# Moving the low-half subtraction of split weights from GpSimd to VectorE in a hybrid transformer block

## The chip, the cores and the metric

The kernel runs on 1 core of one Trainium2 chip. The metric is the device time of one execution in microseconds; of several runs the median counts. Each engine (TensorE for matrix products, VectorE, ScalarE, GpSimd, and the queues that start DMAs) works through its own list of instructions in order and waits on semaphores for the others.

## What is computed

One layer of a diffusion backbone over 512 latent tokens and 256 context tokens with model width 1024, in float32: a modulated RMS norm, one wide input projection that feeds two mixers, a merge, and a mixture of 16 experts. Cut to what matters:

```python
h_c = modulate(ctx, norm1_g, mod_c[0], mod_c[1]);  h_x = modulate(x, norm1_g, mod_x[0], mod_x[1])
qkv_c, z_c, al_c, be_c, cq_c, ckv_c, kr_c, gt_c = split(h_c @ w_in)     # and the same for h_x
# A: short convolution on q, k, v, then a gated delta rule in chunks, both directions, 8 heads
m = where(strict, einsum(k_beta, k) * decay, 0);  t_inv = triangular_solve(m + eye, eye)
# B: latent attention; k and v of all 768 tokens come from rms_norm(c_kv) @ w_ukv, queries from rms_norm(c_q) @ w_uq
x_mid = x + mod_x[2] * ((sigmoid(g_a) * (y_a @ w_out_a) + sigmoid(g_b) * (y_b @ w_out_b)) @ w_o)
out = x_mid + mod_x[5] * expert_choice_moe(modulate(x_mid, ...), router_w, w_gate, w_up, w_down)
```

## The kernel before

**The split.** Up to the router the matrix products keep float32 precision with operands in a reduced type (fp32r): a weight `raw` is split into a high half `wh` (a copy rounded to fp32r) and a low half `wl` (`raw` minus `wh`), and `mm3` (L139 to L142) makes three products of them, `wh` by high input, `wh` by low input, `wl` by high input. `load_split` (L332 to L339) does it for one weight tile of 128 x 1024 elements: a DMA from the SP queue brings `raw` (L336), ScalarE writes `wh` (L337), and L338 writes `wl` on the engine `lo_eng`, or on GpSimd where none is given. The tags `raw`, `whi` and `wlo` have two buffers each, so at most two weights are on their way, and the ScalarE copy of the next but one waits until TensorE has finished with the oldest.

**Who calls it.** `proj` (L521) calls it without an engine, and stands behind `head_k`, `head_q`, `head_v`, `head_z` (eight heads each) and `spill` (the compressed query `cq`, three tiles, the compressed key `ckv`, two, and the merge gates `gt`, sixteen). The first four weights (`k0`, `q0`, `v0`, `k1`) are split by `split_first` (L372) instead, on a GpSimd pinned by name. `load_wkv` (L1110) calls `load_split` without an engine, four times. `branch` (L1404) calls it with `nc.vector`. `load_wq` (L1101) has a GpSimd subtraction of its own. The weight of decays and rotary keys, `abw`, is split at L518 and L519.

**Order.** The program is written as generators (jobs), one for each head and step. `_Emit.step` (L102) runs them by rank and by a planner's estimates of cost and latency, and so sets the order in which instructions are traced; the tile framework then fixes the order on each engine before the run, and the chip keeps it. In the delta-net stage three kinds of job are mixed: projections with convolution (`conv`, L615: on VectorE one product at L623 and four multiply-adds at L626 for each segment, then SiLU on ScalarE at L628, then transposes on TensorE at L635), the chunk preparation (`decay` and `use`, L746 to L782), the inverse of the triangular matrices (`inverse`, L795: 31 steps of L811 and L813 on VectorE, two transposes, then TensorE at `pY`), and the scan over chunks (`scan`, L912, whose VectorE steps are L934, L957, L977, L987, L989). The projections of the gates `gt` and of `z` fill TensorE in between. The attention follows, then the merge and the output projection, then the experts (L1698 to L1788), which stream all expert weights from memory.

Of the kernel before, what the change touches and what calls it, by code (L numbers as in the profile page):

```python
# [11 lines left out]
F32 = mybir.dt.float32  # L12
# [162 lines left out]
def hybrid_block(ctx: ExitStack, tc: tile.TileContext, I, out, dbg=None):  # L175
    nc = tc.nc
# [70 lines left out]
    abw = gp.tile([P, KT, 96], F32, name="abw")  # L247
# [84 lines left out]
    def load_split(src, kt, m, name, lo_eng=None, tiles=None):  # L332
        raw, wh, wl = tiles or (st.tile([P, kt, m], F32, tag="raw", name=f"raw_{name}", **RAW),
                                st.tile([P, kt, m], F32R, tag="whi", name=f"wh_{name}", **WB),
                                st.tile([P, kt, m], F32R, tag="wlo", name=f"wl_{name}", **WB))
        issued[name] = nc.sync.dma_start(raw, src).ins  # L336
        nc.scalar.activation(wh, raw, AF.Copy)  # L337
        (lo_eng or nc.gpsimd).tensor_sub(wl, raw, wh.bitcast(F32))  # L338
        return wh, wl  # L339

    em = _Emit()
# [174 lines left out]
    abh = st.tile([P, KT, 96], F32R, tag="whi", name="abh")  # L516
    abl = st.tile([P, KT, 96], F32R, tag="wlo", name="abl")
    nc.scalar.activation(abh, abw, AF.Copy)  # L518
    nc.gpsimd.tensor_sub(abl, abw, abh.bitcast(F32))  # L519

    def proj(c0, m, name, ctx_=False, w=None):  # L521
        pl = None
        if name in first:
            w, pl = first[name]
        wh, wl = w or load_split(w_in[:, :, c0:c0 + m], KT, m, name)
        begun = pl is not None
        pl = pl if begun else pmm([P, 512], f"pl_{name}")
        pc = pmm([P, 256], f"pc_{name}") if ctx_ else None
        for k in range(KT, KT) if begun else range(KT):
            mm3(nc, pl[:m], wh[:, k], wl[:, k], hx(k, 0), hx(k, 1), k == 0, k == KT - 1)  # L530
            if k % 2:
                yield 1.3, 0, None
        if ctx_:
            for k in range(KT):
                mm3(nc, pc[:m], wh[:, k], wl[:, k], hc(k, 0), hc(k, 1), k == 0, k == KT - 1)
                if k % 4 == 3:
                    yield 1.3, 0, None
        return pl, pc
# [571 lines left out]
    def load_wkv(p):  # L1110
        WKV[p] = load_split(w_ukv[:, :, p * 512:(p + 1) * 512], 2, 512, f"ukv{p}")
        held.append(p)
# [291 lines left out]
    def branch(i, nm, Y, dt, gr):  # L1404
        if not PRM["sl"]:
            nc.scalar.activation(gr, gr, AF.Sigmoid)
        wh, wl = load_split(I[f"w_out_{nm}"][0].rearrange("(k p) c -> p k c", p=P)[:, :, dt * P:(dt + 1) * P],
                            KT, P, f"wo{nm}{dt}", nc.vector if PRM["wv"] or dt % 2 else nc.gpsimd,
                            spare if (nm, dt) == ("a", PRM["da"]) else None)
        yield 0, 2, None  # L1410
        if PRM["sl"]:
            nc.scalar.activation(gr, gr, AF.Sigmoid)
        pa = pmm([P, SEQ], f"pm{nm}{dt}")
        for k in range(KT):
            y = Y[k // 2][:, k % 2]
            mm3(nc, pa, wh[:, k], wl[:, k], y[:, 0], y[:, 1], k == 0, k == KT - 1)
            if k % 2:
                yield 1.3, 0, None
        return pa
# [393 lines left out]
```

## Time and profile before

| | us |
|---|---|
| median of 3 runs | 1807.21 |
| lowest, highest of them | 1804.39, 1810.33 |
| the profiled execution, its own time | 1812.11 |
| its span, first to last instruction | 1810.4 |

Busy shares of the span: TensorE 89%, VectorE 49%, ScalarE 33%, GpSimd 21%. The span falls into a first part up to about 66 us (loads, norms, first weights), the delta-net stage with the projections up to about 720 us, the attention up to about 930 us, the merge and output projection up to about 1065 us, output and routing up to about 1170 us, and the experts. In the names of the profile PE is TensorE, PEld its weight loads, DVE is VectorE, ACT ScalarE and POOL GpSimd. A number in square brackets behind an instruction is the idle time of its engine just before it, with what ended it.

### The profile page before, as it was taken

How to read it: one execution, taken by the hardware profiler on the slowest of the kernel's cores; microseconds unless marked ns; L12 is line 12 of the kernel's file. 1: busy time of each engine (PE TensorE's matmuls, PEld its weight loads, DVE VectorE, ACT ScalarE, POOL GpSimd, SP SyncE). 2: the span in 40 equal slices, each digit the busy share in tenths (PEclk: the TensorE clock that was granted, in tenths of full speed). 3: DMA queues.
4: the chain of work that ended last, by engine and by line, in shares of the span. 5: the costliest groups of instructions: out<-in, count | busy, mean ns of one | idle time of the engine just before them, and what ended most of it. 6: DMA issues, size and time to landing. Idle time of an engine off the chain costs nothing.

```text
span 1810.4 us, 25319 instructions
## 1 busy us (share of the span) xinstructions
PE 1609.5 (89%) x9990; PEld 1107.8 (61%) x9990; DVE 887.6 (49%) x1903; ACT 593.6 (33%) x1336; POOL 380.2 (21%) x380
## 2 busy tenths in 40 slices
PE   5898998898789998699979897999999999999897
PEld 4676797777677787567867785544454444444343
DVE  3677956965896962557774436212122121222122
ACT  4557337425635343456665424100010000000000
POOL 2443433323333423421230442000000000000000
PEclk8999998999989998899989999999999999999999
DMA  9111311243221342131024972799999999999997
GB/s 311 50 47 47 88 42 47 70 143 115 51 73 53 87 156 60 53 102 46 7 88 137 300 258 116 282 414 388 413 384 414 412 413 413 413 414 412 414 413 301
DMA packets 168409, 382.31 MB, mean 211 GB/s; under 512 B 10373, under 2 KB 91491, under 8 KB 168291
## 3 DMA queue, kind: packets, MB, share of 16 engines
q1 hardware_dynamic: 163328, 372.98, 55.6%
q10 hardware_dynamic: 4963, 7.72, 1.3%
q8 instruction: 78, 1.28, 0.3%
q14 instruction: 40, 0.33, 0.1%
HBM read 366.51 MB, written 14.16 MB: 210 GB/s over the span
## 4 chain that ended last, share of the span: by engine, by line
PE 55%; DVE 20%; DMA 9%; ACT 7%; POOL 4%; issue 4%; SPq 0%; ACTq 0%; DVEq 0%; POOLq 0%
PE pd L1765 8%; PE pg L1724 6%; PE pu L1724 5%; DMA wd<-in_w_down_dram 4%; PE pg L1725 3%; DVE tmp L811 3%; PE pu L1725 2%; DVE cy L626 2%; DVE inv L813 2%; DVE qk L626 2%; PE pc L1781 2%; PE pxe L1667 1%; PE pY L170 1%; DVE qv L626 1%; PE pxe L1668 1%
## 5 line engine op out<-in xcount | busy, mean ns | idle before, releaser
L1724 PE MATMUL pg<-w_gate,XE 128*64 128x320 f32 x496 | 183.4, 522 | 0.0
L1724 PE MATMUL pu<-w_up,XE 128*64 128x320 f32 x480 | 159.6, 487 | 2.2 <-DMA w_up<-in_w_up_dram 2.2
L1725 PE MATMUL pg<-w_gate,XE 128*64 128x320 f32 x496 | 161.2, 465 | 0.0
L1745 DVE TENSOR_TENSOR hd<-hd,pu 128x320 f32<-128x320 f32 (+1 forms) x48 | 18.7, 416 | 288.9 <-PE pu L1725 271.7
L1765 PE MATMUL pd<-wd,hd 128*64 128x512 f32 x668 | 152.3, 603 | 1.9 <-DMA wd<-in_w_down_dram 1.9
L1725 PE MATMUL pu<-w_up,XE 128*64 128x320 f32 x480 | 153.9, 444 | 0.0
L1770 ACT ACTIVATE yo<-hd 128x512 fp32r<-128x512 f32 x16 | 10.1, 629 | 342.7 <-DVE hd L1769 342.7
L1724 PEld LDWEIGHTS pu<-w_up,XE 128*64 128x64 f32 x480 | 64.8, 137 | 72.4 <-issue 39.6
L1765 PEld LDWEIGHTS pd<-wd,hd 128*64 128x64 f32 x668 | 45.2, 137 | 86.0 <-issue 78.5
L1724 PEld LDWEIGHTS pg<-w_gate,XE 128*64 128x64 f32 x496 | 67.9, 144 | 47.6 <-issue 28.9
L1725 PEld LDWEIGHTS pg<-w_gate,XE 128*64 128x64 f32 x496 | 61.6, 143 | 24.2 <-issue 11.2
L1743 ACT ACTIVATE hd<-pg 128x320 f32<-128x320 f32 (+1 forms) x48 | 16.5, 378 | 174.9 <-PE pg L1725 174.9
L1781 PE MATMUL pc<-yo 64*128 64x512 f32 x256 | 47.5, 457 | 26.0 <-ACT yo L1770 22.7
L1781 PEld LDWEIGHTS pc<-yo 64*128 64x128 f32 x256 | 23.3, 194 | 67.4 <-ACT yo L1770 35.9
L1785 DVE TENSOR_TENSOR xm<-xm,pc 128x512 f32<-128x512 f32 x72 | 45.9, 682 | 33.7 <-PE pc L1781 33.7
L811 DVE TENSOR_TENSOR tmp<-inv 128x31 f32<-128x31 f32 (+15 forms) x124 | 60.5, 488 | 2.1
L1769 DVE SCALAR_TENSOR_TENSOR hd<-pd,gs,m 128x512 f32<-128x512 f32 x16 | 12.0, 750 | 96.4 <-PE pd L1765 96.4
L626 DVE SCALAR_TENSOR_TENSOR cy<-cx_v,CW,cy 128x510 f32<-128x510 f32 (+3 forms) x64 | 55.6, 886 | 0.2
L140 PE MATMUL pl_gt<-ht,wh_gt 128*128 128x512 f32 x128 | 53.8, 420 | 0.0
L142 PE MATMUL pl_gt<-ht,wl_gt 128*128 128x512 f32 x128 | 51.6, 404 | 2.3 <-POOL wl_gt L338 2.3
L1671 ACT ACTIVATE XE<-pxe,mod,gs 128x256 f32<-128x256 f32 x32 | 16.3, 561 | 113.6 <-PE pxe L1668 101.0
L813 DVE TENSOR_TENSOR inv<-inv,tmp 128x31 f32<-128x31 f32 (+15 forms) x124 | 51.3, 413 | 2.2
(623 smaller groups left out, 4324.3 us busy)
## 6 DMA issues: line engine op xcount, KB each, us to landing
w_gate<-in_w_gate_dram SPq DMA_DIRECT2D x60, 1408.0 KB, 16.2
w_up<-in_w_up_dram SPq DMA_DIRECT2D x60, 1408.0 KB, 17.9
wd<-in_w_down_dram SPq DMA_DIRECT2D x45, 1536.0 KB
aw<-in_ada_w_dram SPq DMA_DIRECT2D x32, 512.0 KB, 5.4
wd<-in_w_down_dram SPq DMA_DIRECT2D x15, 1024.0 KB, 14.0
aq<-in_ada_w_dram SPq DMA_DIRECT2D x8, 1024.0 KB, 9.5
raw_gt<-in_w_in_dram SPq DMA_DIRECT2D x16, 512.0 KB, 3.9
ring_w<-in_w_up_dram SPq DMA_DIRECT2D x3, 1408.0 KB, 11.9
```

The lines of the kernel that those rows point to most:

```text
L140: nc.tensor.matmul(out, wh, xh, start=first, stop=False)
L142: nc.tensor.matmul(out, wl, xh, start=False, stop=last)
L170: return self._tc.keep_in_program_order(f(*a, **kw))
L626: nc.vector.scalar_tensor_tensor(y[:, o + a:o + b], x[:, o + a + j - 2:o + b + j - 2], w(j), y[:, o + a:o + b], op0=OP.mult, op1=OP.add)
L811: nc.vector.tensor_mul(tv, R[:, j + 1:32, j:j + 1].to_broadcast([P, n, j + 1]), X[:, j:j + 1, 0:j + 1].to_broadcast([P, n, j + 1]))
L813: nc.vector.tensor_sub(X[:, j + 1:32, 0:j + 1], X[:, j + 1:32, 0:j + 1], tv)
L1724: nc.tensor.matmul(dst[c][0:64, :n], x_, w[kk][:, o:o + n], start=(k == ko[0]), stop=(k == ko[3] + 1))
L1725: nc.tensor.matmul(dst[c][64:128, :320], x_, w[kk][:, FA + c * 320:FA + c * 320 + 320], start=(k == ko[0]), stop=(k == ko[3] + 1))
L1745: nc.vector.tensor_mul(hd[pr, o:o + b - a], hd[pr, o:o + b - a], pu[c][pr, a:b])
L1765: nc.tensor.matmul(pd[64 * dh:64 * dh + 64], l_, w[:, j, dh * 512:(dh + 1) * 512], start=(i == 0), stop=(i == 10))
L1781: nc.tensor.matmul(pcs[dh], o_[ps_, t, :], y_[ps_, l, :], start=(i + l == 0), stop=(i + l == len(ys_)))
L1785: nc.vector.tensor_add(xm[t][:, sl], xm[t][:, sl], pcs[dh])
```

## The change

The engine for the low half is VectorE instead of GpSimd where `load_split` is given none, and for `abl`:

```diff
@@ load_split
         issued[name] = nc.sync.dma_start(raw, src).ins
         nc.scalar.activation(wh, raw, AF.Copy)
-        (lo_eng or nc.gpsimd).tensor_sub(wl, raw, wh.bitcast(F32))
+        (lo_eng or nc.vector).tensor_sub(wl, raw, wh.bitcast(F32))
         return wh, wl
@@
     nc.scalar.activation(abh, abw, AF.Copy)
-    nc.gpsimd.tensor_sub(abl, abw, abh.bitcast(F32))
+    nc.vector.tensor_sub(abl, abw, abh.bitcast(F32))
```

## Rows read from the trace of the kernel before

**Rows 1.** The page: busy us by engine; VectorE's busy tenths in 40 slices.

```profile
PE 1609.5 (89%) x9990; PEld 1107.8 (61%) x9990; DVE 887.6 (49%) x1903; ACT 593.6 (33%) x1336; POOL 380.2 (21%) x380
...
DVE  3677956965896962557774436212122121222122
```

**Rows 2.** The page: the chain that ended last, by engine.

```profile
PE 55%; DVE 20%; DMA 9%; ACT 7%; POOL 4%; issue 4%; SPq 0%; ACTq 0%; DVEq 0%; POOLq 0%
```

**Rows 3.** Busy time by stage: columns are named in the first line.

```profile
core 0: us, PE busy (x) PEld busy (x) DVE busy (x) ACT busy (x) POOL busy (x), PEclk, DMA share, GB/s
...
66.00:720.00 654.00, 582.20 (x4434) 486.91 (x4432) 476.21 (x1062) 312.53 (x732) 240.67 (x257) 0.94 0.25 75
...
1170.00:1811.00 641.00, 589.09 (x3204) 276.85 (x3202) 140.35 (x292) 37.30 (x85) 0.00 (x0) 0.97 1.00 401
```

**Rows 4.** Line 338 on GpSimd: durations in ns, shortest/median/longest, first and last start.

```profile
L338 POOL TENSOR_TENSOR wl_gt<-raw_gt,wh_gt x16: 2346/2406/3347, 326.3 to 623.2; 128x1024 fp32r<-128x1024 f32 x16
```

**Rows 5.** Groups of VectorE instructions of line 338: busy, mean ns, idle before.

```profile
L338 DVE TENSOR_TENSOR wl_wob<-raw_wob,wh_wob 128x1024 fp32r<-128x1024 f32 x8 | 11.5, 1436 | 11.1 <-ACT wh_wob L337 11.1
...
L338 DVE TENSOR_TENSOR wl_woa<-raw_woa,wh_woa 128x1024 fp32r<-128x1024 f32 x7 | 9.3, 1328 | 12.7 <-ACT wh_woa L337 12.7
```

**Rows 6.** Line 338 alone in the delta-net stage, busy on DVE and POOL.

```profile
66.00:720.00 654.00, 0.00 (x0) 124.51 (x50) 0.94 0.25 75
```

**Rows 7.** Timeline of GpSimd, the subtractions of 310 to 331 us: start, duration.

```profile
310.45 2.47 POOL L338 TENSOR_TENSOR wl_q<-raw_q,wh_q 128x1024 fp32r<-128x1024 f32 x1
...
320.82 2.40 POOL L338 TENSOR_TENSOR wl_v<-raw_v,wh_v 128x1024 fp32r<-128x1024 f32 x1 [7.90 <-ACT wh_v L337]
326.32 2.42 POOL L338 TENSOR_TENSOR wl_gt<-raw_gt,wh_gt 128x1024 fp32r<-128x1024 f32 x1 [3.10 <-ACT wh_gt L337]
```

**Rows 8.** Timeline of VectorE in the same stretch.

```profile
310.60 2.87 DVE L626 SCALAR_TENSOR_TENSOR cy<-cx_v,CW,cy 128x510 f32<-128x510 f32 x1
...
320.88 2.42 DVE L813 TENSOR_TENSOR inv<-inv,tmp 128x60 f32<-128x60 f32 x1
...
326.43 2.60 DVE L626 SCALAR_TENSOR_TENSOR qk<-cx_k,CW,qk 128x255 f32<-128x255 f32 x1
...
329.16 0.47 DVE L626 SCALAR_TENSOR_TENSOR qk<-cx_k,CW,qk 128x255 f32<-128x255 f32 x1
```

**Rows 9.** VectorE, the first and the last prolonged instruction of the stage.

```profile
69.38 2.06 DVE L623 TENSOR_SCALAR qv<-cx_q,CW 128x512 f32<-128x512 f32 x1
...
637.06 2.41 DVE L842 COPY W<-inv 32x192 f32<-32x192 f32 x1
```

**Rows 10.** VectorE by line: durations in ns, shortest/median/longest.

```profile
L626 DVE SCALAR_TENSOR_TENSOR cy<-cx_v,CW,cy x64: 468/737/2919, 78.5 to 515.0; 128x510 f32<-128x510 f32 x16, 128x511 f32<-128x511 f32 x16, 128x254 f32<-128x254 f32 x16, 128x255 f32<-128x255 f32 x16
...
L813 DVE TENSOR_TENSOR inv<-inv,tmp x124: 190/360/2648, 173.4 to 627.7; 128x31 f32<-128x31 f32 x8, 128x60 f32<-128x60 f32 x8, 128x87 f32<-128x87 f32 x8, 128x112 f32<-128x112 f32 x8
...
L775 DVE SCALAR_TENSOR_TENSOR W<-GH,bp,D x96: 331/340/352, 133.1 to 568.0; 128x128 f32<-128x128 f32 x96
```

**Rows 11.** TensorE's waits from 66 to 720 us: total us, times, longest.

```profile
PE ptn_k L635 <- ACT qk L628: 10.0, 5, 3.2
PE ptn_v L635 <- ACT cy L628: 7.4, 4, 2.4
PE pY L168 <- DVE inv L819: 6.8, 3, 4.1
...
PE pl_z L142 <- POOL wl_z L338: 4.5, 2, 3.3
...
PE ptn_q L635 <- ACT qv L628: 3.4, 2, 2.9
...
PE pl_gt L142 <- POOL wl_gt L338: 2.3, 1, 2.3
PE pl_v L142 <- POOL wl_v L338: 1.9, 1, 1.9
```

**Rows 12.** Timeline of TensorE, the wait that closes the stretch of rows 7 and 8.

```profile
331.19 0.48 PE L635 MATMUL ptn_k<-cst,qk 128*128 128x128 f32 x1 [3.06 <-ACT qk L628]
```

## The prediction

> **What bounds the kernel now.** I read the page first. TensorE is busy 89% of the span, VectorE 49%, GpSimd 21%, and the digits show that VectorE's load lies in the first half [rows 1]. In the chain of work that ended last TensorE has 55%, VectorE 20%, GpSimd 4% [rows 2]: an engine that is busy half the time carries a fifth of the end, one that is moved away from carries little. The busy times by stage say where [rows 3]. The experts (1170 us to the end, 641 us) have 1.00 DMA share, TensorE 589 us and no GpSimd at all: nothing of the change happens there, and they start when the work before them is done. The delta-net stage (66 to 720 us, 654 us) has TensorE busy 582 us, VectorE 476, GpSimd 241. So TensorE is idle for 72 us of this stage, and since its order is fixed, what the stage can gain is what these 72 us give back. The list of TensorE's waits says who makes them [rows 11]: mostly results of the convolution on VectorE (10.0, 7.4 and 3.4 us, through a short SiLU on ScalarE), the inverse on VectorE (6.8 us), and the low halves themselves on GpSimd (4.5, 2.3 and 1.9 us).
>
> **What the change removes.** 54 subtractions leave GpSimd: 16 `gt`, 8 `z`, 7 each of `v` and `q`, 6 `k`, 3 `cq`, 2 `ckv`, 4 `ukv`, and `abl`. Fifty of line 338 lie in the delta-net stage and take 124.5 us there [rows 6], 2.4 us each [rows 4]. GpSimd's own time is worth little; what matters is what happens on VectorE meanwhile. At 326.32 us a subtraction of 2.42 us begins on GpSimd; at 326.43 a multiply-add of 128x255 begins on VectorE and takes 2.60 us, and 2.7 us later one of the same shape takes 0.47 [rows 7, 8]. The same at 320.88 (2.42 us for a step whose line has a median of 0.36) and at 310.60 (2.87 against 0.74) [rows 8, 10]. So while GpSimd subtracts, a VectorE instruction with operands in SBUF does not finish: it ends when the subtraction ends, and loses about 2.1 us. Comparing each VectorE instruction that overlaps a subtraction with the shortest of its line and shape, I count 37 that lose over 1 us, from 69.38 us to 637.06 us [rows 9], together 76 us. Instructions that read PSUM are not touched: line 775 stays within 331 to 352 ns over the whole stage [rows 10].
>
> The Trainium skill, "SBUF — State Buffer", section "Who interferes with whom", has a rule for it: VectorE instructions with two SBUF inputs, or in a two-port mode, share a port pair with GpSimd under an exclusive lock, and the later one waits for the whole instruction. The trace agrees (2.60 us against 0.47 us). By that rule the lock works the other way too: a GpSimd instruction that arrives during one of the new VectorE subtractions would wait for it.
>
> **What it adds.** 54 subtractions of 128x1024 on VectorE (`abl` 128x768). The same line runs on VectorE already, in the merge: 1328 ns in the mean for `woa`, 1436 for `wob` [rows 5]. I take 1.33 us. That is 54 x 1.33 = 72 us of new VectorE time against 76 us of stalls that go: VectorE's busy time hardly changes (within about 10 us). The gain is not in the load but in where it lies, and in the shorter way to `wl`.
>
> **The sum, wait by wait.** Between one TensorE wait and the next I count the subtractions and the stalls. A subtraction that stalled VectorE on the way to that wait costs 2.1 us now and 1.33 after, so 0.8 us come back; one that met nothing adds up to 1.33 us; no wait falls below zero.
> Worked once: TensorE waits 3.06 us at 331.19 for the convolution of `k` [rows 12]. On VectorE's way there lie three subtractions, and all three stalled it (2.14, 2.21 and 2.13 us) [rows 7, 8]: 6.5 us go, 3 x 1.33 = 4.0 come, so the wait shrinks by 2.5 us. The same count gives 2.5 at 498.4, 1.6 each at 195.2, 351.3 and 518.5 (two stalls each), 1.5 at 79.3, 1.2 at 177.4, and 0.8 to 0.9 each at 115.9, 159.0, 293.9 and 468.0. Together 16 us of the convolution's waits.
> The inverse: before 220 us four subtractions with three stalls, before 371 us three with two, before 533 us two with one. That is -0.5, -0.3 and +0.7 us, nothing in sum. The scan's waits behind 540 us come out at nothing as well (two that met nothing, three that stalled).
> The direct waits for a low half, 8.7 us [rows 11]: at 699.9 TensorE waits 3.3 us because GpSimd does `ukv`, two additions and then `z`, one after the other. Copy to subtraction takes 0.08 us, so on VectorE these waits shrink by the difference of durations and by the queue: 2.4 and 1.0 us for `z`, 1.2 for `v`, 1.9 for `gt`: 6.5 us.
> Against it, two costs that the trace of before does not show. First, collisions of the new subtractions with what stays on GpSimd: 241 - 125 = 116 us of 654, 18%, so 9 of 50, at 0.1 us (the mean of `wob`, beside which GpSimd works, less that of `woa` [rows 5]) to 1.3 us (GpSimd kept waiting for a whole subtraction): 1 to 12 us of engine time; I take 2, since GpSimd's chain share is 4% [rows 2]. Second, the subtraction now stands in VectorE's order and waits there for the ScalarE copy, with convolution, inverse and scan queued behind it. GpSimd idled 3.1 and 7.9 us for that copy and nobody minded [rows 7]. VectorE's bounds are 0 (the order fixed before the run puts other work first; rows 8 show convolution and inverse steps interleaved singly, so there is other work) and (11.1 + 12.7) / 15 = 1.6 us, its idle time before the 15 subtractions in the merge, where it has little else to do [rows 5]. The stage is closer to the first, as VectorE is busy 73% of it; I take 0.1 us, 5 us over 50, of which the chain's share (20% of 1810 is 362 us, over 888 busy, 0.41) is 2 us.
> The attention's three later `ukv` halves have no TensorE wait behind them: zero.
> Sum: -16 - 6.5 + 2 + 2 = -18.5 us. Against the profiled execution, 1812.1 us by its own time, that is 1793.6. The median of the runs is 4.9 us below it, 1807.2, so the number to compare is **1789 us**, 1.0% less. The later stages keep their length and only start earlier.
>
> **The rivals.**
> *Head-of-line waits on VectorE, slower.* The subtraction stands ahead of the copy it needs, and the copy in turn waits for TensorE to free a `whi` buffer. Then TensorE's filler projections, which nobody waited for, hold up the convolution and the inverse. Price: 50 x (1.33 + 1.6) = 146 us added, 76 removed, +70 on VectorE, times 0.41 on the chain = +29, less the 6.5 us of direct waits: +22, **1829 us**. It decides from about 0.7 us per subtraction: 50 x (1.33 + 0.7) - 76 = 26, times 0.41 = 10, which with the collisions eats the direct waits and more. For it: VectorE is the busiest engine beside TensorE here, and the copies are paced by TensorE. Against: GpSimd's waits for the copy show only that GpSimd was free, not that VectorE will come early.
> The Trainium skill, "Perfetto Trace Analysis", section "Optimizing Scalar/DVE Operations", speaks for this rival: with VectorE saturated, moving work to GpSimd may make sense. It adds itself that the shared port may spoil this; rows 8 show that it does, 2.1 us lost for 1.33 saved.
> *A wash.* The new subtractions land in the same places as the stalls, plus some: busy time -4 us, times 0.41, -2 us; direct waits are taken over by others, since TensorE's order behind them is fixed. **1805 us**, no difference.
> *More than the sum.* VectorE has 654 - 476 = 178 us idle in the stage. If nearly all subtractions fall into it, the convolution's listed waits close (20.8 us), the inverse's (6.8) and the direct ones (8.7), with some of the smaller ones: about -41, **1766 us**.
> *That the change does not do what it says.* The calls with their own engine (`branch`, `split_first`, `load_wq`) stay as they are; the 54 move for certain. No chance of its own.
>
> **How the numbers follow.** Forecast around 1789: 0.46. More than the sum: 0.14. Wash: 0.14. Head-of-line: 0.26. The range runs from 1765 (the large gain) to 1830 (the slow case as priced); beyond lie the worse half of the slow case, some 0.1, and less than 0.1 below. Within 0.3% (5.4 us, about what a measurement of this kernel can tell from no change) is the wash, 0.14; faster is 0.46 + 0.14 = 0.60; slower 0.26.
>
> **What would show it.** Right: lines 626, 811, 813 and 623 have no instructions over about 1.5 us any more; VectorE's busy time in the stage within 10 us of 476; GpSimd's some 240 - 125 = 116; TensorE's waits for `ptn_k`, `ptn_v` and `ptn_q` together at about half of 21 us; waits for `wl` nearly gone. Wrong: VectorE idle before line 338 waiting for line 337 with more than about 35 us in all; TensorE's waits for convolution or inverse unchanged or longer; subtractions of over 1.6 us on VectorE; or a different order of projections that opens new waits.

## The result and the profile after

| | before | after |
|---|---|---|
| median of the runs taken together, us | 1806.81 | 1780.76 |
| lowest, highest | 1804.39, 1810.33 | 1779.32, 1785.01 |
| the profiled execution, its own time | 1812.11 | 1781.53 |
| its span | 1810.4 | 1779.8 |

After stands to before as 0.9858, with a 95% interval of 0.9834 to 0.9882: 26 us less (21 to 30).

The page of the changed kernel, busy time by engine, answers to [rows 1]:

```profile
PE 1597.0 (90%) x9990; PEld 1102.4 (62%) x9990; DVE 877.9 (49%) x1957; ACT 593.2 (33%) x1336; POOL 249.8 (14%) x326
```

GpSimd has 54 instructions fewer and VectorE 54 more. GpSimd has lost 130 us of work. VectorE, which received that work, is busy 10 us less.

Where the time went is read from landmarks that both traces have. The inverse of the first head pair ends at 220.1 us before and at 204.7 after; the second at 371.1 and 352.2; the third at 532.9 and 505.0; the fourth at 632.1 and 605.2. So 15.5, 18.9, 27.9 and 26.9 us are gained by then. The last head pair's output norm (L1001), which ends the delta-net stage, comes 26.8 us earlier (720.5 and 693.7), the output projection starts 29.4 us earlier, the experts' matmuls with the streamed weights 27.3. All of the gain is made before 535 us and then carried along, give or take 3 us. The experts, which the change does not touch, take another 3 us less in these two executions.

Busy time from 66 us to that last norm, the columns as in [rows 3]; the same stretch of the kernel before is 654.5 us long:

```profile
core 0: us, PE busy (x) PEld busy (x) DVE busy (x) ACT busy (x) POOL busy (x), PEclk, DMA share, GB/s
66.00:693.70 627.70, 575.08 (x4431) 482.97 (x4429) 461.28 (x1114) 312.41 (x733) 117.46 (x205) 0.95 0.27 78
```

TensorE's idle time falls from 72.3 us (654.5 - 582.2) to 52.6 (627.7 - 575.1). VectorE's lines, durations in ns as shortest/median/longest, answer to [rows 10]:

```profile
L626 DVE SCALAR_TENSOR_TENSOR cy<-cx_v,CW,cy x64: 468/736/1218, 74.3 to 492.5; 128x510 f32<-128x510 f32 x16, 128x511 f32<-128x511 f32 x16, 128x254 f32<-128x254 f32 x16, 128x255 f32<-128x255 f32 x16
...
L813 DVE TENSOR_TENSOR inv<-inv,tmp x124: 184/360/832, 158.2 to 599.9; 128x31 f32<-128x31 f32 x8, 128x60 f32<-128x60 f32 x8, 128x87 f32<-128x87 f32 x8, 128x112 f32<-128x112 f32 x8
...
L338 DVE TENSOR_TENSOR wl_gt<-raw_gt,wh_gt x16: 1214/1222/1758, 320.5 to 600.0; 128x1024 fp32r<-128x1024 f32 x16
```

The medians are those of before. The longest have come down from 2919 to 1218 ns (L626) and from 2648 to 832 (L813): the stalls are gone. Counted as what each VectorE instruction that overlaps any GpSimd instruction takes above the shortest of its line and shape, where that is over 0.25 us, the stage had 82 us of them and has 7. The subtraction takes 1.22 us here; of the 50 in the stage three take longer than 1.25 us (1.32, 1.76 and 1.79).

The new waits of VectorE for the ScalarE copy, from 66 us to 693.7 (total us, times, longest):

```profile
DVE wl_ukv L338 <- ACT wh_ukv L337: 1.3, 1, 1.3
...
DVE wl_gt L338 <- ACT wh_gt L337: 1.1, 2, 0.9
...
DVE wl_v L338 <- ACT wh_v L337: 0.9, 1, 0.9
DVE wl_k L338 <- ACT wh_k L337: 0.7, 1, 0.7
```

That is 4.0 us in five waits for 50 subtractions: in this stage VectorE rarely comes to a subtraction before its copy is done. Behind the stage the three later `ukv` subtractions wait 9.1 us, but the stretch from the last norm to the first matmul of the merge is no longer for it (228.0 us before, 226.8 after).

TensorE's waits in the same stretch, against [rows 11]:

```profile
PE ptn_k L635 <- ACT qk L628: 10.6, 4, 5.3
...
PE ptn_q L635 <- ACT qv L628: 7.6, 3, 3.4
...
PE pl_z L142 <- DVE wl_z L338: 3.4, 2, 2.8
PE pl_gt L142 <- DVE wl_gt L338: 3.1, 1, 3.1
...
PE pl_q L142 <- DVE wl_q L338: 1.1, 1, 1.1
...
PE ptn_v L635 <- ACT cy L628: 0.6, 2, 0.4
```

Not what one would look for after a gain of 26 us. The convolution's waits have moved between `k`, `v` and `q` (20.8 us before, 18.8 after), and the low halves still keep TensorE waiting for 7.6 us (8.7 before). Only the wait for the inverse, 6.8 us at `pY`, is gone from the list; those for `D` on GpSimd and for the scan's `vn` are shorter (4.3 to 1.7 us, 4.4 to 2.8). The price of the new place can be seen where subtractions stand among the steps of an inverse. VectorE after, start and duration in us:

```profile
318.12 0.76 DVE L626 SCALAR_TENSOR_TENSOR qv<-cx_q,CW,qv 128x510 f32<-128x510 f32 x1
...
319.07 1.24 DVE L338 TENSOR_TENSOR wl_v<-raw_v,wh_v 128x1024 fp32r<-128x1024 f32 x1
320.20 0.40 DVE L811 TENSOR_TENSOR tmp<-inv 128x220 f32<-128x220 f32 x1
320.50 1.24 DVE L338 TENSOR_TENSOR wl_gt<-raw_gt,wh_gt 128x1024 fp32r<-128x1024 f32 x1
321.63 0.40 DVE L813 TENSOR_TENSOR inv<-inv,tmp 128x220 f32<-128x220 f32 x1
```

Two subtractions stand between steps of one inverse, and each puts off what is queued behind it by 1.13 us (from its start to the start of the next). They did not make the wait nearest to them: TensorE waits 3.4 us for the convolution of `q` until 319.70, but VectorE is done with that convolution at 318.88 (first line), before the first subtraction begins. Up to there VectorE had been working on convolution and inverse steps in turn.

### The profile page after: what moved, and what is told of

The parts are those of the page before. It is cut to its first block, busy times and chain, and to the rows that moved or that the text cites. A ratio compares the mean times of both kernels' runs of the same rounds, so it can differ in the third digit from the quotient of the medians.

```text
span 1779.8 us, 25305 instructions
## 1 busy us (share of the span) xinstructions
PE 1597.0 (90%) x9990; PEld 1102.4 (62%) x9990; DVE 877.9 (49%) x1957; ACT 593.2 (33%) x1336; POOL 249.8 (14%) x326
## 4 chain that ended last, share of the span: by engine, by line
PE 40%; DMA 9%; DVE 5%; ACT 2%; issue 2%; POOL 2%; SPq 0%; DVEq 0%; ACTq 0%; POOLq 0%
PE pd L1765 7%; PE pg L1724 6%; PE pu L1724 5%; DMA wd<-in_w_down_dram 4%; PE pg L1725 3%; PE pu L1725 3%; PE pc L1781 2%; DMA w_up<-in_w_up_dram 1%; PE pxe L1667 1%; DMA woraw<-in_w_o_dram 1%; PE pxe L1668 1%; PE pPT L1311 1%; DMA raw_ukv<-in_w_ukv_dram 1%; PE px L140 1%; PE px L142 1%
## 5 line engine op out<-in xcount | busy, mean ns | idle before, releaser
L1724 PE MATMUL pg<-w_gate,XE 128*64 128x320 f32 x496 | 178.6, 511 | 0.0
L1725 PE MATMUL pg<-w_gate,XE 128*64 128x320 f32 x496 | 157.1, 455 | 0.0
L1724 PEld LDWEIGHTS pu<-w_up,XE 128*64 128x64 f32 x480 | 64.6, 137 | 74.3 <-issue 38.1
L140 PE MATMUL pl_gt<-ht,wh_gt 128*128 128x512 f32 x128 | 53.2, 416 | 0.0
L1725 PEld LDWEIGHTS pu<-w_up,XE 128*64 128x64 f32 x480 | 49.8, 135 | 2.8
L141 PE MATMUL pl_gt<-ht,wh_gt 128*128 128x512 f32 x128 | 51.3, 400 | 0.0
L1160 DVE TENSOR_TENSOR PT<-pPT,PT 128x512 fp32r<-128x512 f32 x48 | 33.0, 688 | 24.9 <-ACT PT L1159 24.7
```

Of the source, the lines that this page charges most:

```text
L140: nc.tensor.matmul(out, wh, xh, start=first, stop=False)
L141: nc.tensor.matmul(out, wh, xl, start=False, stop=False)
L1160: nc.vector.tensor_sub(lo, src, hi.bitcast(F32))
L1724: nc.tensor.matmul(dst[c][0:64, :n], x_, w[kk][:, o:o + n], start=(k == ko[0]), stop=(k == ko[3] + 1))
L1725: nc.tensor.matmul(dst[c][64:128, :320], x_, w[kk][:, FA + c * 320:FA + c * 320 + 320], start=(k == ko[0]), stop=(k == ko[3] + 1))
```

## The experiments

The theory is that of the prediction: the time was lost because a GpSimd subtraction holds up VectorE instructions that read SBUF. The rivals for the cause: that GpSimd was simply too slow or too busy (the low half came late, or GpSimd's other work waited behind it), and that nothing was special about the engines, but the planner's order came out luckier. The kernel before, run again beside the experiments, took 1809.1 to 1809.2 us; by the ratio above the changed kernel would stand at 1783.5 there, and "over after" below means over that. All edits are to the changed kernel, most of them to line 338 alone, unless another is named.

**The subtraction back on GpSimd, for nobody.** VectorE makes the low half as in the changed kernel, and GpSimd subtracts once more into the staging buffer, a result that nobody reads:

```diff
-        (lo_eng or nc.vector).tensor_sub(wl, raw, wh.bitcast(F32))
+        (lo_eng or nc.vector).tensor_sub(wl, raw, wh.bitcast(F32)); lo_eng or nc.gpsimd.tensor_sub(raw, wl.bitcast(F32), wh.bitcast(F32))
```

> The changed kernel, and behind each of its new VectorE subtractions in load_split GpSimd does one of the same size too (low half minus high half, written over the raw weight, which nobody reads any more). Nothing else waits for it but the buffer of the raw weight. The order of TensorE, VectorE and ScalarE stays nearly that of the changed kernel. Lock theory: 53 GpSimd subtractions of 2.4 us stall VectorE again by about 2.1 us each where it has an instruction with SBUF operands, 37 to 53 times, 78 to 111 us of VectorE, of which 0.3 to 0.45 end up in the time: 1805 to 1830 us. Rival, order of the instructions: stays at 1781. Rival, the shorter way to the low half: stays at 1781, since the low half is ready as early as before.

Measured: 1837.12 us, 1.0153 of before (1.0137 to 1.0168), 54 us over after. That is above the 1805 to 1830 us expected. The instructions stand in nearly the order of the changed kernel (compared line by line, about a dozen of TensorE's instructions stand elsewhere; between before and after it is about 150). Busy time from 66 us to the last norm, and one line on either engine:

```profile
66.00:747.00 681.00, 587.49 (x4437) 488.26 (x4436) 526.11 (x1117) 314.64 (x736) 242.44 (x256) 0.93 0.25 72
...
L338 POOL TENSOR_TENSOR raw_gt<-wl_gt,wh_gt x16: 2342/2405/2543, 351.4 to 655.2; 128x1024 f32<-128x1024 f32 x16
...
L813 DVE TENSOR_TENSOR inv<-inv,tmp x124: 182/367/2607, 168.5 to 653.8; 128x31 f32<-128x31 f32 x8, 128x60 f32<-128x60 f32 x8, 128x87 f32<-128x87 f32 x8, 128x112 f32<-128x112 f32 x8
```

The stalls are back, 2607 ns at L813, where the changed kernel has 832: 70 us of them in the stage by the count above, 63 more than after. The expectation had 78 to 111 us, of which 0.3 to 0.45 would end up in the time; there are fewer, and 0.85 of them did. VectorE's busy time in the stage rises by 65 us, with as many instructions in the whole program as before (1957). The stage is 53 us longer.

The extra time is not lost on convolution and inverse alone. Here VectorE makes the low halves too, and they come later when it is stalled: TensorE's waits for them grow from 7.6 to 21.8 us (8.2 for `z`, 6.2 for `gt`, 4.0 for `ckv`, 1.8 for `cq`, 1.6 for `q`), and ScalarE's copies wait 53 us for the load of `raw`, where they wait 2 in the changed kernel.

```profile
PE pl_z L142 <- DVE wl_z L338: 8.2, 3, 5.1
```

**The same time on GpSimd without reading.** Three writes of a constant in place of the useless subtraction, about as long together:

```diff
-        (lo_eng or nc.vector).tensor_sub(wl, raw, wh.bitcast(F32))
+        (lo_eng or nc.vector).tensor_sub(wl, raw, wh.bitcast(F32)); lo_eng or [nc.gpsimd.memset(raw.rearrange("p k m -> p (k m)")[:, 0:n], 0.0) for n in (1024, 1024, 512)]
```

> The same place and about the same GpSimd time (0.97 + 0.97 + 0.5 us), but as three memsets over the raw weight, which write SBUF and read nothing. Lock theory, on GpSimd's reads: VectorE is not stalled, 1781 us within 8. If GpSimd being busy were the cost (its other work comes later), or its writes stall VectorE as well: like the kernel with the subtraction, 1805 us or more.

Measured: 1788.01 us, 0.9884 of before (0.9868 to 0.99), 4.5 us over after, within the 8 us expected; its interval overlaps with that of the changed kernel. The same view, and two of VectorE's lines:

```profile
66.00:702.50 636.50, 574.96 (x4429) 480.07 (x4427) 467.07 (x1114) 313.71 (x733) 237.79 (x354) 0.94 0.26 77
...
L338 POOL MEMSET raw_gt<- x48: 518/953/962, 327.6 to 611.0; 128x1024 f32 x32, 128x512 f32 x16
...
L813 DVE TENSOR_TENSOR inv<-inv,tmp x124: 183/359/834, 159.9 to 607.5; 128x31 f32<-128x31 f32 x8, 128x60 f32<-128x60 f32 x8, 128x87 f32<-128x87 f32 x8, 128x112 f32<-128x112 f32 x8
...
L842 DVE COPY W<-inv x64: 241/283/1058, 206.3 to 621.2; 32x192 f32<-32x192 f32 x64
```

GpSimd is busy for 238 us, as long as in the kernel before and within 5 us of the experiment above, yet L813 stays at 834 ns and nearly all of the gain stays. The longest is not even the writes' doing (the instruction on GpSimd at that time is L990, which reads). While one of the writes runs, 104 instructions of L811, L813 and L626 begin, and none of them takes more than 0.07 us above the shortest of its shape; beside a subtraction they lost about 2.1 us.

In both experiments the extra work follows VectorE's subtraction and holds `raw`, in the mean for 3.1 us with the subtraction and for 3.6 with the writes. The useless subtraction also reads, and so holds, `wh` and `wl`, which the expectation left out; ScalarE's copies wait 2.7 us for GpSimd there, against none in the changed kernel. So what the two differ by, 49 us, belongs to the kind of instruction on GpSimd. A busy GpSimd costs little here; one that reads two operands from SBUF costs much.

The writes do hold something: copies with one SBUF operand. The changed kernel's longest L842 is 342 ns, here it is 1058. At 208.89 us three of these copies together take 2.66 us, beside three writes that take 2.55; in the changed kernel three take 0.88. (All stalls of the stage come to 13 us, 5.6 of them at L842.)

**What a subtraction costs on VectorE.** The low half computed twice, both times on VectorE:

```diff
-        (lo_eng or nc.vector).tensor_sub(wl, raw, wh.bitcast(F32))
+        (lo_eng or nc.vector).tensor_sub(wl, raw, wh.bitcast(F32)); lo_eng or nc.vector.tensor_sub(wl, raw, wh.bitcast(F32))
```

> The changed kernel with each of the 53 subtractions done twice on VectorE (same result written again): 65 us more VectorE time, no GpSimd stall. It prices what the moved work itself costs. By the prediction's share (0.41 of VectorE's time is on the chain) +27 us, 1808. If VectorE's idle time takes the subtractions up, +0 to 10 us, 1781 to 1791. If they hold up convolution and inverse for their whole length, up to +65, 1846.

Measured: 1811.74 us, 1.0022 of before (1.0003 to 1.004), 28 us over after: 0.53 us for each of the 53 further subtractions of 1.22 us.

```profile
66.00:718.00 652.00, 584.60 (x4428) 487.73 (x4426) 509.09 (x1163) 312.70 (x733) 124.55 (x204) 0.93 0.25 75
```

VectorE is busy 48 us longer in the stage (the further subtractions add 54, the rest is 7 less). So the subtractions are far from free in their new place: as many again, and the gain is lost. The order shifted more here (about 300 of TensorE's instructions stand elsewhere), so the price per subtraction is rough. But the record has it a second time: the run with the useless subtraction has 53 subtractions on GpSimd, where the kernel before has 54, and 54 on VectorE besides. It is 27.9 us slower than the kernel before, 0.52 us for each, with the other way to the low half in that sum.

**Which subtractions.** One half of them on either engine, then the other way round (with VectorE and GpSimd exchanged in the second line). `abl` stays on VectorE; `filler` stands inline in the kernel. The run with the heads moved came first, so the expectation for the fillers knows its result:

```diff
+        filler = name[:2] in ("gt", "cq", "ck") or name[0] == "z"
-        (lo_eng or nc.vector).tensor_sub(wl, raw, wh.bitcast(F32))
+        (lo_eng or (nc.vector if filler else nc.gpsimd)).tensor_sub(wl, raw, wh.bitcast(F32))
```

> The other part alone: the 29 subtractions of gt, z, cq and ckv on VectorE, with abl; those of k, q, v and ukv on GpSimd. TensorE's order lies nearer to that of the kernel before. If the two parts add up, what the part with the heads alone (1791) left is what this one gains: 1809 - 7.5 = 1801. Lock theory by the share of stalls (45 of 76 us): 1793. Rival, the gain is the order that comes with the heads: 1809, no change.

> Of the changed kernel only the projections of k, q, v, the ukv weights and abl subtract on VectorE; the 29 of gt, z, cq and ckv are back on GpSimd. TensorE's and ScalarE's order is nearly that of the changed kernel. Lock theory: the 29 stalled VectorE 21 times or so for 45 of the 76 us, so 45 us of stalls come back for 35 us of subtractions that go; by the share of stalls 15 of the 26 us are lost, 1796. Rival, order: 1781, as the order is kept. Rival, heads alone matter: 1781.

Measured: with the fillers `gt`, `z`, `cq`, `ckv` on VectorE 1792.95 us, 0.9898 of before (0.9874 to 0.9921); with the heads' `k`, `q`, `v` and `ukv` there 1790.99, 0.989 (0.9856 to 0.9923). Either half brings 16 to 18 us, together 34, while the whole change brings 26: the halves overlap. The landmarks show how. With the heads moved, 13 us are gained by the first inverse and 23 by the third, but only 12 remain at the fourth. With the fillers moved, 0.5 us is gained by the first inverse, 9 by the third and 17 by the fourth. Stalls that are left, 51 us with the heads moved and 38 with the fillers moved, would then eat at another place what was won before; that is read from one execution of each and was not tested.

**The order.** A planner's factor that scales the estimated latency of the delta-net jobs, changed in both kernels:

```diff
-PRM = dict(... ld=1.22, ...)
+PRM = dict(... ld=1.30, ...)
```

> The kernel before with the planner's latency factor for the delta-net jobs at 1.30 instead of 1.22: the same work, some 265 rows of TensorE's order differ. It shows what another order alone does. Mechanism theory: within 10 us of 1809, and the changed kernel with the same factor stays 18 us or more below it. Rival, order: moves by as much as the change itself, 20 us or more, or the difference between the two vanishes.

> The changed kernel with the planner's factor at 1.30, to stand beside the kernel before with the same factor. Mechanism theory: 18 to 35 us below that one. Rival, order: within 10 us of it.

> The kernel before with the planner's latency factor at 1.15: a second other order, some 460 rows of TensorE differ. At 1.30 the kernel before lost 7 us and the difference of the two kernels was 29 us. Mechanism theory: the changed kernel with 1.15 is again 18 to 35 us below this one, wherever this one lies (1795 to 1825). Rival, order: the difference leaves that range.

> The changed kernel with the factor at 1.15, to stand beside the kernel before with the same factor. Mechanism theory: 18 to 35 us below it. Rival, order: within 10 us of it.

| factor | before, us | after, us | difference |
|---|---|---|---|
| 1.30 | 1802.18 | 1773.45 | 28.7 |
| 1.22 | 1809.2 | 1783.5 | 25.7 |
| 1.15 | 1812.47 | 1784.81 | 27.7 |

The 1783.5 is worked out as above; the rest is measured. The order alone is worth 10 us among the three kernels before and 11 among the three after, but the change is worth 26 to 29 us under each of three orders. (The interval of the changed kernel at 1.30, 0.9765 to 0.9844 of before, is some 7 us to either side.) And the stalls go each time: 81 us to 7 with 1.30, 80 to 5 with 1.15. So luck of the order is not what made the gain.

**More of GpSimd's subtractions.** The same move for the first four weights (`split_first`), for `load_wq`, for the low halves in the merge, and for the merge's sums:

```diff
-        GP.tensor_sub(w[1], raws[j], w[0].bitcast(F32))
+        VE.tensor_sub(w[1], raws[j], w[0].bitcast(F32))
...
-            nc.gpsimd.tensor_sub(WQ[p][:, 1, k0:k0 + n], raw, ...
+            nc.vector.tensor_sub(WQ[p][:, 1, k0:k0 + n], raw, ...
...
-            (nc.gpsimd if k % 2 or nm == "b" else nc.vector).tensor_sub(y[:, :, 1], raw, ...
+            nc.vector.tensor_sub(y[:, :, 1], raw, ...
...
-            (nc.gpsimd if k % 4 else nc.vector).tensor_sub(w2[:, :, 1], raw, ...
+            nc.vector.tensor_sub(w2[:, :, 1], raw, ...
...
-PRM = dict(... me=7, ...)
+PRM = dict(... me=0, ...)
```

> The changed kernel with nearly all other float subtractions moved to VectorE too: the first four weights, the query weights of the attention, the low halves of the branch outputs and of the output weights, and the sums and low halves of the merge. Lock theory: in the merge GpSimd stalls VectorE's subtractions by 0.2 to 0.9 us each (1.5 to 2.2 us against 1.22), and its additions and subtractions of 1.3 to 2.4 us lie on the chain there with some 14 us in the kernel before; on VectorE they take 0.7 to 1.3 us. 1770 to 1779 us. Rival, VectorE is full: 1783 or more.

Measured: 1769.58 us, 0.9779 of before (0.9757 to 0.9801): 14 us under the changed kernel, and faster than both. The gain does not lie where the expectation put it, in the merge. The two profiled executions are 12 us apart. By the landmarks some 5 us of that come up to the last norm of the delta net and 9 in the attention, which runs from that norm to the first merge matmul in 218 us, 227 after the change; the merge itself gives 4 of them back (207 us to the experts' first streamed weight, 203 after the change). The attention of the changed kernel has only 3.5 us of stalls by the count above, and here 0.9, so stalls that go are not most of these 9 us; what is was not tested.

**Both together.** The same with the factor 1.30:

> The version with the merge's and the other subtractions on VectorE (1770 us) and the planner's factor at 1.30, which gave the changed kernel 10 us. If the two gains lie in different stages (the factor acts in the delta-net stage, the other behind it) they add: 1760 us. If not, 1765 to 1770.

Measured: 1769.62 us, 0.9775 (0.9746 to 0.9803). The 10 us that the factor brought by itself do not come on top. The delta net is left about as early as with the factor alone (38.5 and 39.4 us before the old kernel) and 6.6 us earlier than without the factor, but the experts start only 2 us earlier than without it. The attention takes back most of the difference: 221.7 us from the last norm to the first merge matmul, 218.0 without the factor. Which work sets its end was not settled.

## Why the prediction was right, point by point

**The place and the cause: right.** Forecast 1789 us, range 1765 to 1830, faster with 0.60; measured 1780.76, faster by 1.4%. The stalls [rows 7, 8] were the cause: gone in the changed kernel (L813 at 832 ns), back with the useless subtraction (2607 ns, 54 us), absent at L813 with writes of about the same length in sum (834 ns, 4.5 us). The Trainium skill, "SBUF — State Buffer", section "Who interferes with whom", says that a VectorE instruction with two SBUF inputs contends with a GpSimd instruction that reads SBUF, not with one that only writes it, and that a copy can enter a mode in which it contends for the shared ports as a whole. The runs agree with all three: 2607 ns at L813 beside the subtraction, at most 0.07 us lost by 104 instructions of L811, L813 and L626 that began beside a write, and 1058 ns at the copy L842 beside the writes.

**The head-of-line rival: rightly put second.** I took 0.1 us a subtraction, 5 us in all; in the stage it came to 4.0. The bound of 1.6 us from the merge [rows 5], where VectorE has little else to do, does not hold in a stage where it is busy 73% of the time. The collisions with GpSimd's remaining work are few too: three of the 50 subtractions stand out, where I counted on nine. Two of them, 1.76 and 1.79 us, are over the 1.6 us that I had named as a sign of being wrong; together they lose 1.1 us. That this stayed small is not the same as free: the subtractions cost 0.53 us each by their own length. The rival's share of 0.41 of VectorE's time gives 0.50 us for 1.22.

**The advice that spoke for the rival.** The Trainium skill, "Perfetto Trace Analysis", section "Optimizing Scalar/DVE Operations", weighs moving VectorE's work to GpSimd where VectorE is saturated, with the shared port as its reservation. Here the reservation decides: 1.22 us saved on VectorE per subtraction, about 2.1 us lost in each that met an instruction.

**The load on VectorE: nearly right.** I expected 476 us in the stage within 10; it is 461. The 50 subtractions there take 1.22 us and not 1.33. Neighbouring instructions overlap by about 0.1 us in the trace, so they add 56 us of busy time, and the rest of VectorE is busy for 71 us less, most of the 75 us of stalls that go: 476 + 56 - 71 = 461.

**The sum of waits: right in its total, wrong in its parts.** I had 18.5 us off TensorE's idle time; it is 19.7 (72.3 to 52.6). That the total agrees so closely is luck, for the step that reached it failed. It went from one TensorE wait to the next and took from each what the stalls and subtractions on the way to it would change, as if every TensorE instruction kept its place. It does not: about 150 of TensorE's instructions stand elsewhere. And where an earlier wait is shortened, the next can be reached sooner and grow; which of the two moved the waits was not separated. So the convolution's waits were to fall by 16 us and fell by 2 on the list, the direct waits for a low half were to fall by 6.5 and fell by 1, and the inverse was to give nothing and lost its 6.8 us. Two of my signs of being right failed with it: the waits for `wl` are not nearly gone (7.6 of 8.7 us), and the convolution's are not halved (18.8 of 20.8); those for `q` grew from 3.4 to 7.6 us, which I had named as a sign of being wrong. The landmarks say it as plainly: by that count, the direct wait for `v` at 171 us included, 8 us should have been gained by the first inverse, 13 by the second and 17 by the third; it was 15.5, 18.9 and 27.9. What comes back up to there was counted 1.5 to 2 times too small, and the direct waits were taken too high. Smaller slips stand in the count itself. Two of its eleven convolution waits are none: that at 115.9 us is a wait of the gates' matmul (L591), and that at 468.0 ends with ScalarE's L669; 1.7 of the 16 us. And by its own rule the inverse comes to about -1.1, -0.3 and +0.5 us, not -0.5, -0.3 and +0.7.

**The terms, as the runs measured them.** A microsecond of stall costs more of the end than one of VectorE's ordinary load: over the changed kernel the useless subtraction made 54 us of 63 us of stall, 0.85, and over the run with writes 49 us of 57, 0.86. In the wash I took 0.41 for everything, in the sum 0.8 us net for each stall on a listed wait's way and nothing for the others. A subtraction on VectorE costs 0.53 and 0.52 us in the two pairs of runs that show it, 0.43 of its length, close to the 0.41 of the chain. Put on the change, 75 us of stalls at 0.85 and 54 subtractions at 0.53 make -64 + 29 = -35, against 26 measured. Here the price of the stalls is the weak term: it comes from a kernel in which the stalled VectorE makes the low halves as well, with 14 us more of TensorE's waits for them, and in the kernel before it made none of these. By the price of the subtractions and the 26 us, the stalls of the kernel before and the longer way to the low half cost 26 + 29 = 55 us together. Why a stall weighs more than load beyond that was not tested; that GpSimd subtracts just when a projection has to move on, with VectorE's next step due, is only argued.

**What the sum left out.** I held TensorE's busy time fixed. It fell by 7.1 us in the stage (582.2 to 575.1) with three matmul records fewer. The granted clock reads 0.94 before and 0.95 after, and by an estimate it explains about half. In the two traces the clock is at the lower of its two levels (1.2 of 2.4 GHz) for 78.5 us of the stage before and for 68.3 after, and TensorE is busy for 68.9 and 59.6 us of that. A matmul of 128x512 (L141) takes 628 ns there and 393 at the upper level, so 9.3 us fewer at the lower level give back about 3.5 us (9.3 less 9.3 x 393 / 628). The other half stays open; the ends of matmuls are modelled. From the profiled execution the forecast was 1793.6 and it took 1781.5. Of these 12 us TensorE's busy time is 7, the idle time beyond the sum 1, and most of the rest the experts' 3 us, which no step of the change reaches and which the spread of the runs covers.

**The wash and the larger gain.** The wash is out: the interval ends at 0.9882. The larger gain, 1766 us, put nearly all waits of convolution, inverse and low halves at zero; they stand at 26 us, so the changed kernel did not go that way.

## What to carry to other kernels

In this kernel the lost time stood in no list of VectorE's waits. Where a line's longest duration is far above its median and its excess matches the length of a GpSimd instruction that runs at the time, a stall is to be suspected, and it hides in the busy time; the same work put back beside it, and then writes of the same length in its place, showed it to be one. So read minimum, median and maximum of VectorE's lines before believing a busy share. Work with SBUF operands that is moved to GpSimd to relieve VectorE can cost VectorE more than it relieves; compare what the operation takes there (1.22 us) with what it takes away (2.1 us a hit, and how many hit). A count of waits one by one gave the wrong parts here and the right total by luck: where the order is planned anew, idle time that goes at one wait can come back at another.

## What was not expected of the hardware

The prediction had neither of two things. Copies with one SBUF operand are held by GpSimd's writes while two-operand steps are not: L842 went from 342 to at most 1058 ns, about the length of one write (953 ns), and L813 stayed at 834. And the subtraction takes 1.22 us in this stage against 1.33 and 1.44 in the merge [rows 5], where GpSimd works beside it: the new place is cheaper than the nearest rows said.
